# A gated recurrence in levels: the products of two levels issued as one run, one of them from copies of its operands

## The chip, the cores and the metric

The kernel runs on one core of a Trainium2 chip. The metric is the device time of one execution in microseconds; the time of a version is the median of several runs. All arithmetic is in float32, some of it in the form float32r in which a weight is split into a high and a low part and multiplied in three products. The engines are TensorE (PE in the profile, its weight loads PEld), VectorE (DVE), ScalarE (ACT), GpSimd (POOL) and SyncE (SP, which issues the DMAs).

## The reference

Two layers of a decoder trunk over 512 tokens of 1024 features. Each layer normalises, projects, runs two groups of heads side by side and projects back. The part that the change touches is the first group, a gated linear recurrence with 8 heads of 128 x 128 state:

```python
def step(state, xs):                     # one chunk; b = cumulated log decay
    qch, kch, vch, b = xs
    diff = b[:, :, :, None, :] - b[:, :, None, :, :]
    decay = jnp.where(causal, jnp.exp(jnp.where(causal, diff, 0.0)), 0.0)
    scores = jnp.einsum('bhtd,bhsd,bhtsd->bhts', qch, kch, decay)
    o = jnp.einsum('bhts,bhsv->bhtv', scores, vch)
    o = o + jnp.einsum('bhtd,bhdv->bhtv', qch * jnp.exp(b), state)
    ...
```

The second group is sliding-window attention with 16 heads. Both are gated, concatenated, projected by w_out, normalised and added to x.

## The kernel before

**Stages.** Each layer is a list of projection slabs (q, k and v of the attention, values, gates and queries of the recurrence, output gates, and the output projection in four parts: a0, a1, h0, h1). A slab's weights come in pieces of 128 x 512 over the sync queue (L163), are split on ACT (L183, the high part) and on DVE (L184, the low part), and are multiplied on TensorE (L295). `step` issues one step of a unit: three matmuls of 512 columns. At most two units run at a time, and three PSUM banks `pj` hold their sums; a unit may begin when its bank has been drained by its `evac`, on ACT or DVE (for the part a0 of the output projection: the copy to y, L901).

**Streams.** `merge` interleaves such a projection stream with a stream of other work, by the weights that the streams yield: whatever yields a larger number is followed by more projection steps. TensorE executes in the order of issue. `pin` keeps an instruction in program order; what is not pinned may be moved by the scheduler on its engine.

**The recurrence.** It is computed for four heads at a time (`hgrn(0)` and `hgrn(4)` in each layer, so four groups in all; two heads lie side by side in one "pair", a tile of 2 x 512 tokens). The lower triangle of scores is built in levels of hh = 2, 4, 8, 16, 32, 64 tokens: within each block of 2 hh tokens, the keys k of the first half meet the queries q of the second half. At each level TensorE does the products of both pairs into two PSUM banks `sc` (L764 for levels up to 16, L769 for level 32, L773 for level 64); then the halves are scaled by the decay of the neighbouring half, q on DVE (L780) and k on POOL (L781), in place, so that the next level finds its operands; and the products are moved into the tile of scores, on DVE with a mask (L788) or, for levels 32 and 64, on ACT (L793, eight pieces for both pairs; L798, four). The three `sc` banks go round. Each level issues two yields of 3.0.

**Before and behind.** `prepare(a)` makes the operands of the first diagonal blocks: for the first two heads of a group in two buffers of the tag "b" (two of them exist, 2 x 512 elements per partition each), with a reciprocal, two products and two copies (L735 to L744). `spread(a)` (L711) multiplies them. In the first merge of a layer, `prepare(2)`, `hgrn(0)` and `prepare(4)` are one chain; in the next, `prepare(6)` and `hgrn(4)`. Behind the levels come transposes of k (L807), states (L819) and outputs (L832, L835). The tag "b" is also used by the attention and by the gains of the norms (`load_g`, L366, on the sync queue).

Of the kernel before, what the change touches and what calls it, by code (L numbers as in the profile page):

```python
# [20 lines left out]
NT = SEQ // 128  # L21
# [50 lines left out]
def hybrid_kernel(ctx: ExitStack, tc: tile.TileContext, x, xt, wkv, win, wout, g_pre, g_post, lbp, ghead, sinks,  # L72
# [12 lines left out]
    def pin(ins):  # L85
        return tc.keep_in_program_order(ins)
# [8 lines left out]
    def sc():  # L95
        sc_turn[0] += 1
        return sc_tiles[sc_turn[0] % SC]

    def ac():
        ac_turn[0] += 1  # L100
        return ac_tiles[ac_turn[0] % len(ac_tiles)]
# [257 lines left out]
    def halves(tag):  # L359
        t = tmp(tag, n=2)  # L360
        return [t[:, 0], t[:, 1]]
# [73 lines left out]
    def layer(l, last):  # L435
# [310 lines left out]

        def hgrn(a):
            two = [quad.pop(a), quad.pop(a + 2)]
            bank = ac()
            spread(a, bank)  # L750
            keep_spread(a, bank)
            yield 3.0
            for hh in (2, 4, 8, 16, 32, 64):
                nb = SEQ // (2 * hh)
                per, qu = nb // NT, nb // NT // 4
                Ls = [sc(), sc()]
                for (k, q, _), L in zip(two, Ls):
                    qv = q.rearrange("p (b two j) -> p b two j", two=2, j=hh)
                    for m in range(2 * NT):
                        o_ = m * P  # L760
                        if hh <= 16:
                            for b in range(4):
                                blk, c = m * per + b * qu, m * 64 + 16 * b
                                pin(nc.tensor.matmul(L[32 * b:32 * b + 32, c:c + 16], lhsT=k[:, o_ + 32 * b:o_ + 32 * b + 32],  # L764
                                                     rhs=qv[:, blk:blk + qu, 1, :], start=True, stop=True, tile_position=(0, 32 * b)))
                        elif hh == 32:
                            for b in range(2):
                                s_, r_, c = o_ + 64 * b, 64 * b + 32 * (m % 2), m // 2 * 32
                                pin(nc.tensor.matmul(L[r_:r_ + 32, c:c + 32], lhsT=k[:, s_:s_ + 32],  # L769
                                                     rhs=q[:, s_ + 32:s_ + 64], start=True, stop=True, tile_position=(0, r_)))  # L770
                        else:
                            b, c = m % 2, m // 2 * 64
                            pin(nc.tensor.matmul(L[64 * b:64 * b + 64, c:c + 64], lhsT=k[:, o_:o_ + 64],  # L773
                                                 rhs=q[:, o_ + 64:o_ + 128], start=True, stop=True))
                for i, ((k, q, _), L) in enumerate(zip(two, Ls)):
                    h = a + 2 * i
                    qv = q.rearrange("p (b two j) -> p b two j", two=2, j=hh)
                    kv_ = k.rearrange("p (b two j) -> p b two j", two=2, j=hh)
                    tv = tots[h].rearrange("p (b two) -> p b two", two=2)
                    nc.vector.tensor_tensor(qv[:, :, 1, :], qv[:, :, 1, :], tv[:, :, 0].unsqueeze(2).broadcast_to([P, 2 * nb, hh]), op=ALU.mult)  # L780
                    nc.gpsimd.tensor_tensor(kv_[:, :, 0, :], kv_[:, :, 0, :], tv[:, :, 1].unsqueeze(2).broadcast_to([P, 2 * nb, hh]), op=ALU.mult)  # L781
                    tots[h] = sm.tile([P, 2 * nb], F32, tag=f"tot{hh}", name=f"tot{hh}", bufs=2)
                    nc.vector.tensor_tensor(tots[h], tv[:, :, 0], tv[:, :, 1], op=ALU.mult)
                    A = pairs[h].rearrange("p i t -> p (i t)")
                    if hh <= 16:
                        Av = A.rearrange("p (n b two j) -> p n b two j", n=2 * NT, two=2, j=hh)[:, :, :, 1, :]
                        mv = lmask[hh].rearrange("p (b j) -> p b j", j=hh).unsqueeze(1).broadcast_to([P, 2 * NT, per, hh])
                        nc.vector.copy_predicated(Av, mv, L.rearrange("p (n b j) -> p n b j", n=2 * NT, j=hh))  # L788
                    elif hh == 32:
                        Av = A.rearrange("p (m two t) -> p m two t", m=NT, two=2)  # L790
                        for b in range(2):
                            for e in range(2):
                                nc.scalar.copy(Av[64 * b:64 * b + 32, :, e, 64 * b + 32:64 * b + 64],  # L793
                                               L[64 * b + 32 * e:64 * b + 32 * e + 32, 0:128].rearrange("p (m t) -> p m t", m=NT))
                    else:
                        Av = A.rearrange("p (m b t) -> p m b t", m=NT, b=2)
                        for b in range(2):
                            nc.scalar.copy(Av[0:64, :, b, 64:128],  # L798
                                           L[64 * b:64 * b + 64, 0:256].rearrange("p (m t) -> p m t", m=NT))
                    yield 3.0  # L800

            kps = []
            for j in range(4):
# [430 lines left out]
```

## Time and profile before

| | |
|---|---|
| runs of the kernel before | median 909.93 us of 3, 909.6 to 910.25 |
| the profiled execution | 909.04 us |
| span of its trace | 907.3 us |
| records on L764, L769, L773 (TensorE) | 2048, 256, 128 |
| records on L711 | 512 |

A float32 product leaves two matmul records, so L769 has 32 products per group (two pairs, eight blocks of 128 tokens each, two per block), L773 has 16, and L711 and each level of L764 have 64.

A page of the profile shows busy time per engine, the granted clock of TensorE in tenths, and the chain of work that ended last. The timeline lists instructions by start, with the duration and, in brackets, the idle time of the engine before them and who ended it. "x64" at a row's end says that 64 records are merged in it. Matmuls overlap in the pipeline, so their starts tell more than their durations.

### The profile page before, as it was taken

The page shows a single profiled execution, that of the slowest core. Times are in us where ns is not written, and L with a number is a line of the kernel's source. Part 1 is how long each engine was busy: PE and PEld are TensorE (multiplying, and loading weights), DVE is VectorE, ACT ScalarE, POOL GpSimd, SP SyncE. Part 2 cuts the span into 40 slices and gives each one's busy share as a digit, 9 for nine tenths or more (in the row PEclk, how much of TensorE's full clock was granted, in tenths as well). Part 3 has the DMA queues.
Part 4 walks back from the last instruction along what each step waited for, and adds up shares of the span by engine and source line. Part 5 has one row for each costly group of instructions (what it writes and reads, how often), then busy time and mean ns, then how long its engine had stood idle before and what let it go on. Part 6 is the DMA issues. An engine that isn't in the chain of part 4 may idle for free.

```text
span 907.3 us, 18589 instructions
## 1 busy us (share of the span) xinstructions
PE 895.5 (99%) x7206; PEld 746.4 (82%) x7206; DVE 655.2 (72%) x1179; ACT 464.4 (51%) x1051; POOL 254.7 (28%) x233
## 2 busy tenths in 40 slices
PE   9999999999999999999999999999999999999997
PEld 7888888888888878887888888888888888888885
DVE  5878987989946885655787787877778457666556
ACT  7636767654656323534463376686346463135242
POOL 0135544204313122121332344550134121230102
PEclk9999999999999999999999999999999999999999
DMA  9684712322222421334356556222312323213414
GB/s 323 212 215 130 197 49 68 105 94 83 72 82 80 130 82 48 94 117 129 99 178 189 150 154 172 62 72 89 116 57 86 96 70 106 72 48 95 138 35 139
DMA packets 57144, 102.82 MB, mean 113 GB/s; under 512 B 6624, under 2 KB 9184, under 8 KB 57056
## 3 DMA queue, kind: packets, MB, share of 16 engines
q1 hardware_dynamic: 56768, 101.50, 37.0%
q8 instruction: 57, 0.93, 0.5%
q14 instruction: 31, 0.25, 0.1%
q10 hardware_dynamic: 288, 0.14, 0.1%
HBM read 89.03 MB, written 12.58 MB: 112 GB/s over the span
## 4 chain that ended last, share of the span: by engine, by line
PE 87%; DVE 7%; ACT 2%; DMA 1%; issue 1%; POOL 1%; POOLq 0%; DVEq 0%; ACTq 0%
PE pj L295 70%; PE ac L629 3%; PE sc L572 2%; PE sc L764 2%; PE sc L603 1%; PE ac L832 1%; PE ac L1060 1%; DMA raw<-in_wkv_dram 1%; DVE wlo L184 1%; PE ac L819 1%; PE ac L835 1%; PE sc L885 1%; PE sc L559 1%; DVE y L905 1%; PE sc L807 1%
## 5 line engine op out<-in xcount | busy, mean ns | idle before, releaser
L183 ACT CAST whi<-raw 128x512 fp32r<-128x512 f32 x256 | 156.0, 621 | 130.2 <-PE pj L295 118.8
L184 DVE TENSOR_TENSOR wlo<-raw,whi 128x512 fp32r<-128x512 f32 x253 | 180.8, 733 | 38.6 <-ACT whi L183 37.3
L295 PE MATMUL pj<-hhi,wlo 128*128 128x512 f32 x512 | 202.3, 396 | 0.0
L295 PE MATMUL pj<-hhi,whi 128*128 128x512 f32 x512 | 199.9, 390 | 0.0
L295 PE MATMUL pj<-hlo,whi 128*128 128x512 f32 x512 | 199.5, 390 | 0.0
L295 PE MATMUL pj<-whi,ops 128*128 128x512 f32 (+1 forms) x520 | 173.1, 395 | 0.2 <-DVE ops L865 0.2
L295 PEld LDWEIGHTS pj<-whi,ops 128*128 128x128 f32 x520 | 97.2, 188 | 20.0 <-DVE ops L865 0.6
L295 PEld LDWEIGHTS pj<-hhi,whi 128*128 128x128 f32 x512 | 96.1, 188 | 20.6
L295 PEld LDWEIGHTS pj<-hhi,wlo 128*128 128x128 f32 x512 | 96.1, 188 | 19.5
L295 PEld LDWEIGHTS pj<-hlo,whi 128*128 128x128 f32 x512 | 96.2, 188 | 18.9
L295 PE MATMUL pj<-whi,hlo 128*128 128x512 f32 x256 | 103.5, 406 | 0.3 <-DVE y L905 0.3
L295 PE MATMUL pj<-wlo,ops 128*128 128x512 f32 (+1 forms) x260 | 100.9, 388 | 0.5 <-ACT ops L864 0.5
L295 PE MATMUL pj<-wlo,hhi 128*128 128x512 f32 x256 | 100.4, 392 | 0.4 <-DVE wlo L184 0.3
L295 PE MATMUL pj<-whi,hhi 128*128 128x512 f32 x256 | 100.3, 392 | 0.0
L781 POOL TENSOR_TENSOR k<-k,tot 128x512 f32<-128x512 f32 x40 | 57.5, 1456 | 115.1 <-PE sc L764 45.9
L590 ACT ACTIVATE s<-sc,negm 128x128 f32<-128x128 f32 x128 | 45.6, 368 | 37.5 <-DVE negm L583 35.2
L295 PEld LDWEIGHTS pj<-wlo,ops 128*128 128x128 f32 x260 | 49.0, 188 | 9.5 <-ACT ops L864 0.9
L295 PEld LDWEIGHTS pj<-whi,hhi 128*128 128x128 f32 x256 | 48.1, 188 | 10.4
L295 PEld LDWEIGHTS pj<-wlo,hhi 128*128 128x128 f32 x256 | 48.3, 189 | 8.9 <-DVE wlo L184 1.2
L295 PEld LDWEIGHTS pj<-whi,hlo 128*128 128x128 f32 x256 | 48.2, 188 | 8.6 <-DVE y L905 0.7
L597 POOL TENSOR_TENSOR s<-s,sums 128x512 f32<-128x512 f32 x32 | 35.2, 1101 | 51.7 <-DVE sums L595 27.7
L780 DVE TENSOR_TENSOR q<-q,tot 128x512 f32<-128x512 f32 x40 | 41.7, 1056 | 10.7 <-PE sc L769 4.7
(209 smaller groups left out, 1383.8 us busy)
## 6 DMA issues: line engine op xcount, KB each, us to landing
raw<-in_win_dram SPq DMA_DIRECT2D x192, 256.0 KB, 2.8
raw<-in_wout_dram SPq DMA_DIRECT2D x64, 256.0 KB, 2.7
stack<-rot SPq DMA_DIRECT2D x16, 512.0 KB, 3.4
qs<-stack SPq DMA_DIRECT2D x32, 256.0 KB, 4.7
xs<-in_xt_dram SPq DMA_DIRECT2D x8, 256.0 KB, 4.4
raw<-in_wkv_dram SPq DMA_DIRECT2D x8, 256.0 KB, 4.1
a<-in_x_dram SPq DMA_DIRECT2D x8, 256.0 KB, 3.9
x_mid<-a SPq DMA_DIRECT2D x8, 256.0 KB, 3.4
```

Of the source, the lines that this page charges most:

```text
L183: keep(nc.scalar.copy(hi, v))
L184: keep((nc.gpsimd if i in on_pool and i % 2 else nc.vector).tensor_tensor(lo, v, hi.bitcast(F32), op=ALU.subtract))
L295: nc.tensor.matmul(u.o, lhsT=u.sta(k, u.w)[i], rhs=u.mov(k, u.w)[j], start=(n == 0), stop=(n == len(u.list) - 1))
L559: pin(nc.tensor.matmul(S[:, h * P:(h + 1) * P], lhsT=q[:, h, t_], rhs=kst[v][p][:, 0:P], start=(h == 0 and p == 0), stop=(h == 3 and p == 1)))
L572: pin(nc.tensor.matmul(S[:, h * 256:(h + 1) * 256], lhsT=q[:, 2 * hp_ + h, t_], rhs=kst[v][p][:, (n - 1) * P:(n + 1) * P], start=(h == 0 a ...
L590: nc.scalar.activation(pt[:, h * P:(h + 1) * P], cur[h], AF.Exp, bias=negm[:, h:h + 1], scale=SCALE, accum_out=sums[:, h:h + 1])
L597: nc.gpsimd.tensor_tensor(pv, pv, sums.unsqueeze(2).broadcast_to([P, 4, P]), op=ALU.mult)
L603: pin(nc.tensor.transpose(T[:, h * P:(h + 1) * P], pt[:, h * P:(h + 1) * P], ident))
L629: pin(nc.tensor.matmul(U, lhsT=vst[v][:, blk, :], rhs=d, start=(i == 0), stop=(i == len(terms) - 1)))
L764: pin(nc.tensor.matmul(L[32 * b:32 * b + 32, c:c + 16], lhsT=k[:, o_ + 32 * b:o_ + 32 * b + 32], rhs=qv[:, blk:blk + qu, 1, :], start=True ...
L780: nc.vector.tensor_tensor(qv[:, :, 1, :], qv[:, :, 1, :], tv[:, :, 0].unsqueeze(2).broadcast_to([P, 2 * nb, hh]), op=ALU.mult)
L781: nc.gpsimd.tensor_tensor(kv_[:, :, 0, :], kv_[:, :, 0, :], tv[:, :, 1].unsqueeze(2).broadcast_to([P, 2 * nb, hh]), op=ALU.mult)
```

## The change

At level 32 nothing is multiplied any more. ACT copies the first halves of k and the second halves of q of each pair into a buffer of the tag "b" (`kept`, one for each pair: 128 x 512 elements of k, as many of q), and the scaling of k and q goes on. At level 64 the 16 products of that level are issued as before, and behind them, in the same run, the 32 products of level 32, from the copies. They go into columns 256 to 383 of the same two banks, and all twelve evacuations of ACT follow there. The yields are 2.0 at level 32 and 4.0 at level 64 instead of 3.0 at each, so that their sum stays.

```diff
         def hgrn(a):
             two = [quad.pop(a), quad.pop(a + 2)]
+            kept = []
...
-                Ls = [sc(), sc()]
+                Ls = [sc(), sc()] if hh != 32 else [None, None]
                 for (k, q, _), L in zip(two, Ls):
+                    if hh == 32:
+                        kept.append(halves("b"))
+                        for t, x, e in zip(kept[-1], (k, q), (0, 1)):
+                            nc.scalar.copy(t.rearrange("p (b j) -> p b j", j=hh), x.rearrange("p (b two j) -> p b two j", two=2, j=hh)[:, :, e, :])
+                        continue
...
-                        elif hh == 32:
-                            for b in range(2):
-                                s_, r_, c = o_ + 64 * b, 64 * b + 32 * (m % 2), m // 2 * 32
-                                pin(nc.tensor.matmul(L[r_:r_ + 32, c:c + 32], lhsT=k[:, s_:s_ + 32],
-                                                     rhs=q[:, s_ + 32:s_ + 64], start=True, stop=True, tile_position=(0, r_)))
                         else:
                             b, c = m % 2, m // 2 * 64
                             pin(nc.tensor.matmul(L[64 * b:64 * b + 64, c:c + 64], lhsT=k[:, o_:o_ + 64],
                                                  rhs=q[:, o_ + 64:o_ + 128], start=True, stop=True))
+                if hh == 64:
+                    for (k, q), L in zip(kept, Ls):
+                        for m in range(2 * NT):
+                            for b in range(2):
+                                s_, r_, c = 64 * m + 32 * b, 64 * b + 32 * (m % 2), 256 + m // 2 * 32
+                                pin(nc.tensor.matmul(L[r_:r_ + 32, c:c + 32], lhsT=k[:, s_:s_ + 32], rhs=q[:, s_:s_ + 32],
+                                                     start=True, stop=True, tile_position=(0, r_)))
...
-                    elif hh == 32:
+                    elif hh == 64:
                         Av = A.rearrange("p (m two t) -> p m two t", m=NT, two=2)
                         for b in range(2):
                             for e in range(2):
                                 nc.scalar.copy(Av[64 * b:64 * b + 32, :, e, 64 * b + 32:64 * b + 64],
-                                               L[64 * b + 32 * e:64 * b + 32 * e + 32, 0:128].rearrange("p (m t) -> p m t", m=NT))
-                    else:
+                                               L[64 * b + 32 * e:64 * b + 32 * e + 32, 256:384].rearrange("p (m t) -> p m t", m=NT))
                         Av = A.rearrange("p (m b t) -> p m b t", m=NT, b=2)
...
-                    yield 3.0
+                    yield {32: 2.0, 64: 4.0}.get(hh, 3.0)
```

Lines behind the edit move by up to seven: the levels up to 16 are L770 now, level 64 is L774 and the products from the copies are L781, the copies themselves L762, the scalings L788 and L789, the evacuations L801 and L805, the y copy L908.

How the order of instructions moves is shown in two places of the first group of the first layer. First TensorE, before: the run of level 32 between steps of the projections (`pj` are their banks, `sc2` and `sc0` two of the three banks of the recurrence).

```order
L295 MATMUL pj_2751<-hlo_122,whi_2582 128x512
L295 MATMUL pj_2751<-hhi_121,whi_2582 128x512
L769 MATMUL sc2_80<-q_1933,k_1803 32x32 x16
L769 MATMUL sc0_78<-q_2126,k_2032 32x32 x16
L295 MATMUL pj_2865<-whi_2710,ops_2228 128x512
```

And the run of level 64, which stands 33 projection matmuls behind it:

```order
L295 MATMUL pj_2976<-wlo_2604,ops_2227 128x512
L295 MATMUL pj_2976<-whi_2603,ops_2227 128x512
L773 MATMUL sc1_79<-q_1933,k_1803 64x64 x8
L773 MATMUL sc2_80<-q_2126,k_2032 64x64 x8
L295 MATMUL pj_2953<-whi_2725,ops_2228 128x512
```

Now, the joined run (`b` are the two buffers of copies):

```order
L295 MATMUL pj_2927<-wlo_2604,ops_2227 128x512
L295 MATMUL pj_2927<-whi_2603,ops_2227 128x512
L774 MATMUL sc2_80<-q_1933,k_1803 64x64 x8
L774 MATMUL sc0_78<-q_2126,k_2032 64x64 x8
L781 MATMUL sc2_80<-b_2893 32x32 x16
L781 MATMUL sc0_78<-b_2896 32x32 x16
L295 MATMUL pj_2911<-whi_2725,ops_2228 128x512
```

It stands 21 projection matmuls behind the place that the run of level 32 left, and 45 ahead of the transposes of k; one run of projections is no longer cut.

Second, ACT, before, from the conversions ahead of level 32 to the first y copies (`k_2626` and `q_2854` belong to the heads that `prepare(4)` prepares, `a` are the tiles of scores, `y` takes the output projection):

```order
L688 ACTIVATE f_2625<-f_2625,lb_b_136,lb_a_135 128x512
L738 COPY b_3378<-k_2626 128x256
L183 CAST whi_2871<-raw_2723 128x512
L183 CAST whi_2886<-raw_2830 128x512
L696 ACT_TABLE_LOAD
L696 ACTIVATE q_2854<-q_2854 128x512
L736 COPY b_3338<-q_2854 128x256
L793 COPY a_1983<-sc2_80 32x4x32 x4
L793 COPY a_2168<-sc0_78 32x4x32 x4
```

Now the same place, where the four copies stand and no evacuation:

```order
L688 ACTIVATE f_2625<-f_2625,lb_b_136,lb_a_135 128x512
L762 COPY b_2893<-k_1803 128x512
L762 COPY b_2893<-q_1933 128x512
L762 COPY b_2896<-k_2032 128x512
L762 COPY b_2896<-q_2126 128x512
L183 CAST whi_2871<-raw_2723 128x512
L183 CAST whi_2886<-raw_2830 128x512
L696 ACT_TABLE_LOAD
L696 ACTIVATE q_2854<-q_2854 128x512
```

And further on, now, behind the joined run:

```order
L908 COPY y_2918<-pj_2865 128x512
L801 COPY a_1983<-sc2_80 32x4x32 x4
L805 COPY a_1983<-sc2_80 64x4x64 x2
L801 COPY a_2168<-sc0_78 32x4x32
L908 COPY y_2995<-pj_2911 128x512
L801 COPY a_2168<-sc0_78 32x4x32 x3
L805 COPY a_2168<-sc0_78 64x4x64 x2
L736 COPY b_3344<-q_2854 128x256
L738 COPY b_3344<-k_2626 128x256
L183 CAST whi_3023<-raw_2869 128x512
L908 COPY y_3016<-pj_2927 128x512
```

The twelve evacuations stand together around the second y copy, and the copies of `prepare(4)` (L736, L738), two of which stood ahead of or between the evacuations, have gone behind them, since their buffers are taken until the joined run has read them. On DVE the reciprocals and products of `prepare(4)` and on POOL its two L742 move behind the scalings of level 64 in the same way. On the sync queue the loads of the norm gains into "b" (L366), which waited for the second group's `spread`, now stand behind thirteen more weight loads and wait for the second group's joined run.

## The prediction

> **What bounds the kernel now.** I read the page first, then the lists of waits, then the timelines of the engines around one group of four heads.
>
> ```profile
> span 907.3 us, 18589 instructions
> PE 895.5 (99%) x7206; PEld 746.4 (82%) x7206; DVE 655.2 (72%) x1179; ACT 464.4 (51%) x1051; POOL 254.7 (28%) x233
> PEclk9999999999999999999999999999999999999999
> PE 87%; DVE 7%; ACT 2%; DMA 1%; issue 1%; POOL 1%; POOLq 0%; DVEq 0%; ACTq 0%
> ```
>
> TensorE (PE) is busy in 99% of the span, its granted clock stays in the top tenth throughout, and 87% of the chain that ended last is its own work. So the change is worth what it does to TensorE's row of matmuls, unless it makes TensorE wait for someone. The lists of waits (who for whom, us in total, times, longest) say how near that is:
>
> ```profile
> POOL k L781 <- PE sc L769: 22.7, 4, 6.4
> PE sc L1037 <- DVE u L1028: 1.5, 1, 1.5
> PE pj L295 <- ACT ops L864: 0.5, 1, 0.5
> ```
>
> POOL stands 22.7 us before the products that are moved, but that costs nothing, since nobody on TensorE waits for POOL there. TensorE's own longest wait is 1.5 us, at the start, and 0.5 us later on.
>
> **What a run of products costs TensorE.** Its timeline in the first group of the first layer (start, duration, engine, line, count):
>
> ```profile
> 236.19 0.39 PE L295 MATMUL pj<-whi,ops 128*128 128x512 f32 x1
> ...
> 238.68 0.39 PE L295 MATMUL pj<-hhi,whi 128*128 128x512 f32 x1
> 239.00 0.76 PE L769 MATMUL sc<-q,k 128*32 128x32 f32 x64
> 239.69 0.50 PE L295 MATMUL pj<-whi,ops 128*128 128x512 f32 x1
> 240.03 0.39 PE L295 MATMUL pj<-wlo,ops 128*128 128x512 f32 x1
> ...
> 241.65 0.62 PE L295 MATMUL pj<-whi,ops 128*128 128x512 f32 x2
> ```
>
> Durations overlap, so only starts count. Projection matmuls (L295) start every 0.226 us: the eleven steps from 236.19 to 238.68 take 2.49. From the last one before the run (238.68) to the second behind it (240.03) pass 1.35 us, of which two ordinary steps are 0.45. The run of level 32 (32 products, 64 records) therefore costs **0.90 us**. Afterwards the seven steps from 240.03 to 241.65 take 1.62, 0.231 each: some 0.04 us more goes into a slow stretch behind the run.
>
> How much of the 0.90 is fixed? The diagonal spread (L711) has twice as many products of the same form, 64, and level 64 (L773) has 16 of 64 columns:
>
> ```profile
> 197.86 0.39 PE L295 MATMUL pj<-hhi,whi 128*128 128x512 f32 x1
> 198.17 0.73 PE L711 MATMUL ac<-b 128*32 128x32 f32 x62
> ...
> 199.44 0.50 PE L295 MATMUL pj<-hhi,wlo 128*128 128x512 f32 x1
> 199.78 0.40 PE L295 MATMUL pj<-hlo,whi 128*128 128x512 f32 x1
> 247.14 0.39 PE L295 MATMUL pj<-whi,ops 128*128 128x512 f32 x1
> 247.45 1.15 PE L773 MATMUL sc<-q,k 128*64 128x64 f32 x32
> 248.54 0.50 PE L295 MATMUL pj<-whi,ops 128*128 128x512 f32 x1
> 248.87 0.39 PE L295 MATMUL pj<-wlo,ops 128*128 128x512 f32 x1
> ```
>
> By the same count L711 costs 1.92 - 0.45 = 1.47 and L773 1.73 - 0.45 = 1.28. Thirty-two more products of the form of L769 cost 1.47 - 0.90 = 0.57, so 0.90 - 0.57 = **0.33 us is the fixed price** of going into a run and out of it.
>
> **The change part by part.** *TensorE.* No product disappears: the 32 of level 32 now read the copies and stand directly behind the 16 of level 64. What goes is one entry and one exit per group (four groups: two per layer). What comes is one change inside the run, from tiles 64 columns wide to tiles 32 wide; no row shows it. Its bounds are 0 (products simply follow products; then 0.33 is saved) and 0.33 (as dear as an exit and an entry together; then nothing is). It is one change of form where exit and entry are two, so I take half, 0.16. With the one slow stretch that also goes: 0.16 + 0.04 = 0.20 per group, **0.8 us in four groups**.
>
> The Trainium skill, page "TensorEngine Tiling (Array Packing)", section "Key Properties", says that changing the tiling mode, and not merely the tile, drains the TensorE. That speaks against the full saving: four changes of mode per group become three. By the rule the sum is a quarter of the two fixed prices, 0.16 per group; by a count of runs alone it would be 0.33. The step of 0.32 instead of 0.226 us from 238.68 to 239.00 agrees that a change of mode costs something.
>
> *ScalarE (ACT)* gets 16 copies, four per group. Nearest rows: a conversion of the same 128x512 elements, and the evacuations that now stand together:
>
> ```profile
> 232.15 0.80 ACT L688 ACTIVATE f<-f,lb_b,lb_a 128x512 f32<-128x512 f32 x1
> 232.85 0.41 ACT L738 COPY b<-k 128x256 f32<-128x256 f32 x1
> ...
> 239.54 2.14 ACT L793 COPY a<-sc 32x128 f32<-32x128 f32 x8 [0.79 <-PE sc L769]
> 241.70 0.62 ACT L183 CAST whi<-raw 128x512 fp32r<-128x512 f32 x1
> ...
> 248.19 1.52 ACT L798 COPY a<-sc 64x256 f32<-64x256 f32 x4
> 249.73 0.59 ACT L901 COPY y<-pj 128x512 f32<-128x512 f32 x1
> ```
>
> At 0.62 us a copy (bounds 0.6 and 0.8 by these rows) that is 2.5 us per group and 10 us in all, on an engine that is idle 49% of the span: nothing, as long as nothing behind it in its queue is late. Are the operands there? The copies need level 16's scaled k from POOL and q from VectorE (DVE):
>
> ```profile
> 230.90 2.93 POOL L781 TENSOR_TENSOR k<-k,tot 128x512 f32<-128x512 f32 x2 [2.71 <-PE sc L764]
> 233.44 0.94 DVE L780 TENSOR_TENSOR q<-q,tot 128x512 f32<-128x512 f32 x1
> 241.01 2.15 DVE L780 TENSOR_TENSOR q<-q,tot 128x512 f32<-128x512 f32 x2
> ```
>
> The second k is ready at 233.8, the second q at 234.4; ACT's queue reaches the copies at about 232.9 and ends them at 235.4. The scalings of level 32 follow (2.15 on DVE, about 2.9 on POOL): done by about 238. The joined run comes 21 projection matmuls behind the old place of L769, at 238.68 + 22 x 0.226 + 0.09 = 243.7. TensorE has some 5 us to spare and will not wait for the copies.
>
> *ACT behind the joined run.* Twelve evacuations now stand together (2.14 + 1.52 = 3.7 us), and the projections' y copies (L901) between and behind them. First bank full at about 245.1; the four L793 and two L798 of it end at 246.9, one L793 and the next y copy at 247.8, the other five evacuations at 249.4; then two copies of prepare (0.41 each), a conversion (0.62) and the third y copy, which ends at about 251.4 (before: 250.3). Its bank is written again by the unit that starts with the second matmul of this row, 253.43, less the 0.2 saved:
>
> ```profile
> 253.20 0.61 PE L295 MATMUL pj<-whi,ops 128*128 128x512 f32 x2
> ```
>
> 1.8 us to spare. The cover is thinner by 1.3 us than it was, and each microsecond beyond it would be one of TensorE's.
>
> *What waits for the "b" buffers.* The kept copies take the two buffers that prepare(4) had used early. Its reciprocals, products and POOL's two L742 move behind the joined run, and so do weight splits (L184) behind them on DVE:
>
> ```profile
> 234.93 1.74 DVE L735 RECIPROCAL b<-f 128x256 f32<-128x256 f32 x1
> 248.80 1.54 DVE L184 TENSOR_TENSOR wlo<-raw,whi 128x512 fp32r<-128x512 f32 x1
> 264.35 0.40 PE L295 MATMUL pj<-hhi,wlo 128*128 128x512 f32 x1
> ```
>
> Two reciprocals and their products put the split of 248.80 back by 2 to 4 us; the slab that it belongs to is first read at 264.35. Nothing. On the sync engine's queue (SP) the loads of the norm gains into "b" move behind thirteen weight loads and wait for the second group's joined run (about 360):
>
> ```profile
> 307.54 0.81 SPq L366 DMA_DIRECT2D b<-in_g_post_dram  x2
> 337.63 31.98 SPq L163 DMA_DIRECT2D raw<-in_wout_dram  x8
> 364.68 0.62 ACT L183 CAST whi<-raw 128x512 fp32r<-128x512 f32 x1 [0.53 <-PE pj L295]
> ```
>
> They stand behind the fifth of those eight loads. The sixth waits for a conversion that comes at 364.7, so the hole is there already. Nothing either.
>
> **Sum.** 0.8 us off the profiled execution's own 909.04 gives 908.2; off the 909.93 of the runs, which lie 0.9 higher, **909.1**.
>
> **Rivals.** *The inner change is free*: all of 0.33 + 0.04 goes, 4 x 0.37 = 1.5, 908.4. For it: products of one form follow each other without a gap; against it: the step into a run is 0.09 us too long. *It costs as much as exit and entry*: only the slow stretch goes, 0.16, 909.8. For it: the new weights have another width and another source than those before. *The products hide under level 64's*: 4 x 0.90 = 3.6, 906.3; against it, TensorE issues one after the other, and no row shows two forms side by side. *ACT's queue becomes the wait*: copies stand in order, so a late q on DVE holds everything behind them. The place is groups one and three, where y copies drain the projections' banks; it decides from 1.8 us of further delay on. In the second layer ACT drains q itself, behind the copies, and DVE's second scaling of q begins late:
>
> ```profile
> 682.80 1.28 ACT L696 ACT_TABLE_LOAD   x1
> 685.97 0.60 ACT L696 ACTIVATE q<-pj 128x512 f32<-128x512 f32 x1 [1.89 <-PE pj L295]
> 686.23 0.68 DVE L780 TENSOR_TENSOR q<-q,tot 128x512 f32<-128x512 f32 x1
> ```
>
> The copy of that q cannot start before 686.9, the table load (1.28) and L696 come after it, some 3 us later than now. If such delays run 1.5 us past the cover in both groups, that is 2 x 1.5 = 3.0 against the gain: 912.1, slower than before. Against it stands the slack worked out above.
>
> **How the numbers follow.** Forecast 0.47; inner change free 0.20, as dear as two 0.20; hidden products 0.05; ACT's queue 0.08. A measurement of this kernel tells about 0.2% (1.8 us) from no change: below 908.1 is faster, above 911.75 slower. The first three cases are all within it: 0.87. Hidden products make faster 0.05, ACT's queue slower 0.08. The range takes in the three cases and 0.2 to 0.5 us at each end, for runs that lie otherwise and small waits: 908.2 to 910.3.
>
> **What would show it.** The joined run, counted as above, should cost 0.90 + 1.28 - 0.16 = 2.0 us (1.85 if the inner change is free, 2.2 if it saves nothing). The step into the run and out of it should be as before, and the projections around it at 0.226. TensorE's busy time should not fall much more than the span. Wrong would be: a gap of TensorE ahead of a projection unit within 15 us behind a joined run, released by ACT; a joined run that starts late, released by ACT or POOL; or POOL's wait for it beyond what its queue had.

## The result, and the profile after

| | runs | median us | range us |
|---|---|---|---|
| before, on the same chip | 13 | 909.60 | 908.50 to 910.31 |
| changed | 13 | 907.51 | 906.93 to 908.91 |

The ratio is 0.9981, with a 95% interval of 0.9974 to 0.9988: the changed kernel is 2.1 us faster, 1.1 to 2.4 by the interval. The forecast was a gain of 0.8 us (909.1, range 908.2 to 910.3). The sign was right, and the gain was more than twice as large. The time lies below the range.

The page of the changed kernel, the rows that answer to those of before:

```profile
span 905.3 us, 18588 instructions
PE 893.1 (99%) x7206; PEld 746.8 (83%) x7206; DVE 652.1 (72%) x1179; ACT 471.7 (52%) x1067; POOL 255.4 (28%) x233
PEclk9999999999999999999999999999999999999999
PE 87%; DVE 6%; issue 3%; ACT 2%; POOL 1%; DMA 0%; POOLq 0%; DVEq 0%; ACTq 0%
```

TensorE has the same 7206 records, the clock is as before, and TensorE's busy time is 2.4 us shorter, as the span is 2.0 shorter. ACT has 16 copies more and is busy 7 us longer. The chain's share of DMA, 1% before, is 0%. TensorE's waits (who for whom, us in total, times, longest):

```profile
PE sc L1044 <- DVE u L1035: 1.5, 1, 1.5
PE sc L393 <- DVE xn L388: 1.1, 2, 0.7
...
PE pj L295 <- ACT ops L871: 0.5, 1, 0.5
PE pj L295 <- DVE wlo L184: 0.3, 1, 0.3
```

No wait for ACT's y copies (L908) or for POOL is among them. The joined run on TensorE's timeline, first group of the first layer:

```profile
236.04 0.39 PE L295 MATMUL pj<-hhi,whi 128*128 128x512 f32 x1
...
243.52 0.39 PE L295 MATMUL pj<-whi,ops 128*128 128x512 f32 x1
243.84 1.15 PE L774 MATMUL sc<-q,k 128*64 128x64 f32 x32
244.92 0.76 PE L781 MATMUL sc<-b 128*32 128x32 f32 x64
245.61 0.50 PE L295 MATMUL pj<-whi,ops 128*128 128x512 f32 x1
245.95 0.39 PE L295 MATMUL pj<-wlo,ops 128*128 128x512 f32 x1
```

From 243.52 to 245.95 pass 2.43 us, less two steps of 0.2275: the run costs **1.975 us**, where two runs cost 0.895 + 1.275 before. The 33 steps ahead of it, from 236.04 to 243.52, take 7.48, or 0.2267 each; they begin with the 21st matmul behind the run of level 16. Before, a run of level 32 stood among them, and the 31 steps behind that run (240.03 to 247.14, rows quoted in the prediction) took 7.11, which is 0.08 more than 31 ordinary ones. They are not slow throughout (first three rows before, last row changed):

```profile
242.11 0.39 PE L295 MATMUL pj<-wlo,ops 128*128 128x512 f32 x1
...
243.70 0.63 PE L295 MATMUL pj<-whi,ops 128*128 128x512 f32 x2
...
245.78 0.62 PE L295 MATMUL pj<-whi,ops 128*128 128x512 f32 x2
```

```profile
248.01 0.39 PE L295 MATMUL pj<-wlo,ops 128*128 128x512 f32 x1
```

The nine steps from 240.03 to 242.11 take 2.08 (0.231 each), the next seven 1.59 (0.227), then nine again 2.08, and the last six 1.36 (0.227). So a slow stretch lasts about ten steps, costs some 0.04 us and is over; the second one here has no run ahead of it, and no row shows what began it. Behind the joined run the nine steps from 245.95 to 248.01 take 2.06, which is 0.02 beyond ordinary ones. ACT at the same place:

```profile
232.56 0.62 ACT L762 COPY b<-k 128x512 f32<-128x512 f32 x1 [0.47 <-POOL k L789]
233.09 0.61 ACT L762 COPY b<-q 128x512 f32<-128x512 f32 x1
234.06 0.62 ACT L762 COPY b<-k 128x512 f32<-128x512 f32 x1 [0.35 <-POOL k L789]
234.58 0.62 ACT L762 COPY b<-q 128x512 f32<-128x512 f32 x1
...
245.45 1.06 ACT L801 COPY a<-sc 32x128 f32<-32x128 f32 x4 [2.94 <-PE sc L781]
246.53 0.74 ACT L805 COPY a<-sc 64x256 f32<-64x256 f32 x2
...
250.79 0.59 ACT L908 COPY y<-pj 128x512 f32<-128x512 f32 x1
```

The copies are done at 235.2, nearly ten microseconds ahead of their readers, and the third y copy ends at 251.38.

**Where the time went, stretch by stretch.** Single matmul starts of TensorE's timeline cut the span into stretches that hold the same work in every version: from one `spread` to the next, to the transposes of zh, the gated output of the recurrence (L885 before, L892 now), to the transposes in the norm of the second layer (L393). The table has three profiled executions of the kernel before (the last two from the experiments) and two of the changed one, in us:

| stretch | before, three executions | changed, two executions |
|---|---|---|
| A: 1st `spread` to 2nd (group 1) | 108.80, 108.80, 108.77 | 108.46, 108.45 |
| B1: to the second transposes of zh (group 2) | 58.87, 58.90, 58.91 | 58.58, 58.59 |
| B2: to the fifth (no products of a group) | 51.01, 50.58, 50.09 | 50.10, 50.10 |
| C1: to the last L393 | 45.62, 45.61, 45.60 | 45.90, 45.90 |
| C2: to the 3rd `spread` (attention, second layer) | 186.52, 186.48, 186.48 | 186.16, 186.15 |
| D: 3rd `spread` to 4th (group 3) | 108.96, 108.95, 108.81 | 108.66, 108.69 |
| E: to the transposes of zh (group 4) | 57.66, 57.80, 57.75 | 57.40, 57.42 |

A, B1, D and E hold the four groups and lose 0.34 + 0.31 + 0.23 + 0.33 = **1.2 us**. The forecast had 0.8 there. B2, C1 and C2 hold no product of the change; by the means they give -0.46 + 0.29 - 0.34 = **-0.5 us**, which the forecast didn't have at all. So two things had to be found out: why joining gives 1.2, and what B2 is. What stands ahead of the first `spread` takes 197.9 to 200.1 us in the nineteen profiles (198.3 and 200.1 in two of one kernel), so a span or a time also moves by that. (The expectations below call the end of B2 the fourth transposes of zh; it is the fifth group of them, at 416.85 us in the kernel before.)

In B2 the profiled execution of before has this on TensorE:

```profile
408.22 0.39 PE L295 MATMUL pj<-whi,hhi 128*128 128x512 f32 x1
408.88 0.50 PE L295 MATMUL pj<-whi,hlo 128*128 128x512 f32 x1 [0.28 <-DVE y L905]
...
411.06 0.39 PE L295 MATMUL pj<-whi,hlo 128*128 128x512 f32 x1
411.48 0.50 PE L295 MATMUL pj<-wlo,hhi 128*128 128x512 f32 x1
```

Two starts are 0.66 and 0.42 apart where 0.2275 is usual, 0.6 us lost, and 0.9 in all with slow steps behind both (B2 is 50.1 without them). The cause is a chain on the other engines (sync queue, ACT, DVE):

```profile
402.24 0.38 SPq L163 DMA_DIRECT2D raw<-in_wkv_dram  x1
402.71 0.42 SPq L938 DMA_DIRECT2D a<-in_x_dram  x1
...
406.29 0.62 ACT L183 CAST wkv<-raw 128x512 fp32r<-128x512 f32 x1 [1.31 <-DMA raw<-in_wkv_dram]
...
406.94 0.69 DVE L184 TENSOR_TENSOR wkv<-raw,wkv 128x512 fp32r<-128x512 f32 x1 [2.04 <-ACT wkv L183]
...
408.15 0.68 DVE L905 TENSOR_TENSOR y<-pj,y 128x512 f32<-128x512 f32 x1
```

The third piece of wkv (a weight of the next layer) lands 4.05 us behind its issue. Its conversion, its low part on DVE and the y sum behind that in DVE's queue are late, and the y sum frees the bank that TensorE wants. In the changed kernel the same load is issued at 401.30 and converted at 404.21.

### The profile page after: what moved, and what is told of

Read it like the earlier page. It is cut to its first block, busy times and chain, and to the rows that moved or that the text cites. A ratio compares the mean times of both kernels' runs of the same rounds, so it can differ in the third digit from the quotient of the medians.

```text
span 905.3 us, 18588 instructions
## 1 busy us (share of the span) xinstructions
PE 893.1 (99%) x7206; PEld 746.8 (83%) x7206; DVE 652.1 (72%) x1179; ACT 471.7 (52%) x1067; POOL 255.4 (28%) x233
## 4 chain that ended last, share of the span: by engine, by line
PE 87%; DVE 6%; issue 3%; ACT 2%; POOL 1%; DMA 0%; POOLq 0%; DVEq 0%; ACTq 0%
PE pj L295 71%; PE ac L629 3%; PE sc L572 2%; PE sc L770 2%; PE ac L839 2%; PE sc L603 1%; PE ac L842 1%; PE ac L826 1%; DVE wlo L184 1%; PE sc L892 1%; PE sc L559 1%; PE sc L814 1%; PE ac L711 1%; DVE a L973 1%; DVE y L912 0%
## 5 line engine op out<-in xcount | busy, mean ns | idle before, releaser
L789 POOL TENSOR_TENSOR k<-k,tot 128x512 f32<-128x512 f32 x40 | 58.3, 1480 | 108.3 <-PE sc L770 51.9
L788 DVE TENSOR_TENSOR q<-q,tot 128x512 f32<-128x512 f32 x40 | 37.4, 946 | 20.3 <-PE sc L774 10.9
```

## The experiments

Medians are compared with the kernel before in the same session (909.1 to 909.3 us in all of them).

### Both kernels again, and the join taken apart

> The kernel before, unchanged, with a second trace. In the first trace TensorE loses 0.9 us (gaps of 0.43 and 0.19 us beyond the usual start to start, and a slow stretch) near 408 us, where the fourth load of the next layer's wkv weights lands late and holds VectorE's queue. Theory A, landing luck: that gap belongs to the execution and not to the kernel; this trace may lack it or have it elsewhere, and its span then goes with it (without it about 906.3 us). Theory B, the change removes it by its order: the gap stands here again at the same place with about the same length, and the span is about 907.3.

> The changed kernel, unchanged, with a second trace. Theory A: the direct gain is 0.3 us per group, 1.2 in all (ratio about 0.9987), and the rest of the first difference comes and goes; this trace may show a gap near 407 us. Theory B: no gap near 407 us, ratio about 0.9977, 2.1 us. In both the joined run costs 1.98 us in the first layer's first group.

Measured: 909.26, ratio 1.0001 (0.9992 to 1.0009), and 907.62, ratio 0.9982 (0.9974 to 0.9991), a gain of 1.7 us. The stall was there again in the kernel before, half as long (B2 50.58), and not in the changed one (50.10). That looked like theory B; the third profile of the kernel before, further below, speaks against it.

`e1_apart` keeps the copies and the places of all else, and puts the products back into a run of their own (and their evacuation with it):

```diff
-                Ls = [sc(), sc()] if hh != 32 else [None, None]
+                Ls = [sc(), sc()]
...
-                if hh == 64:
+                if hh == 32:
                     for (k, q), L in zip(kept, Ls):
...
-                    yield {32: 2.0, 64: 4.0}.get(hh, 3.0)
+                    yield 3.0
```

> As the changed kernel with its copies and its use of the b buffers, but the products of level 32 form a run of their own at their old place again, and its evacuations follow there. If joining the runs is what gains: the direct gain is gone, about +1.2 us against the changed kernel, ratio to the kernel before 0.999 to 1.001. If the copies (POOL and VectorE need no longer wait for TensorE, the b buffers held longer, the loads of the gains moved) are what gains: it stays 1 us or more faster than the kernel before, ratio about 0.998.

Measured: 908.2, ratio 0.9992 (0.9983 to 1.0001). Its runs cost 0.885 and 1.285, as before. Stretches A, B1, D and E lie within 0.15 us of those of before: what they lose in the changed kernel comes with the join, not with the copies. By its time alone this run lies between the two cases, 1.1 us below the kernel before and 0.6 above the changed one: its profile has no stall (B2 50.09) and a C2 as short as the changed kernel's (186.12).

`e1_turns` lets the products of both levels take turns inside the joined run, one of level 64, two of level 32, so that it has 31 changes of width instead of one:

```diff
+                            if hh == 64:
+                                kk, qq = kept[[id(x[0]) for x in two].index(id(k))]
+                                for b in range(2):
+                                    s_, r_, c = 64 * m + 32 * b, 64 * b + 32 * (m % 2), 256 + m // 2 * 32
+                                    pin(nc.tensor.matmul(L[r_:r_ + 32, c:c + 32], lhsT=kk[:, s_:s_ + 32], rhs=qq[:, s_:s_ + 32],
...
-                if hh == 64:
-                    for (k, q), L in zip(kept, Ls):
```

> As the changed kernel, but inside the joined run the 16 products of level 64 and the 32 of level 32 alternate (one, then two): 31 changes of tile width per run in place of one, all else the same. If each change costs what the first trace leaves for it, 0.13 us (fixed price 0.33 less the 0.20 that a joined run saved): a run of 1.98 + 30 x 0.13 = 5.9 us, and about 15 us more in all, 923 us. If a change of width inside a run is free: runs of 1.98 us and no difference, 907.5 us. If TensorE can even overlap products of the two widths: shorter runs, below 1.9 us.

Measured: 930.59, ratio 1.0243 (1.0227 to 1.0259). TensorE's timeline, the ends of the run:

```profile
243.88 0.39 PE L295 MATMUL pj<-whi,ops 128*128 128x512 f32 x1
244.20 0.33 PE L774 MATMUL sc<-q,k 128*64 128x64 f32 x2
244.46 0.26 PE L780 MATMUL sc<-b 128*32 128x32 f32 x4
244.64 0.33 PE L774 MATMUL sc<-q,k 128*64 128x64 f32 x2
...
251.10 0.26 PE L780 MATMUL sc<-b 128*32 128x32 f32 x4
251.29 0.50 PE L295 MATMUL pj<-whi,ops 128*128 128x512 f32 x1
251.62 0.40 PE L295 MATMUL pj<-wlo,ops 128*128 128x512 f32 x1
```

The run costs 7.74 - 0.455 = 7.285 us. Thirty more changes cost 7.285 - 1.975 = 5.31, **0.177 us each**. The expectation had 0.13 for a change and so a time of 923 us; the prediction had taken 0.16 between 0 and 0.33. The Trainium skill's page "TensorEngine Tiling (Array Packing)", section "Key Properties", says that a change of the tiling mode drains the TensorE. This run agrees that a change costs time, and gives the price; whether a drain is what costs it, no row shows.

### The width change taken away

`e2_narrow` computes level 64 in tiles that are 32 columns wide too, 32 products of 64 columns instead of 16, so that the joined run has one width throughout; `e3_narrow_apart` does the same to the kernel before, in the old place:

```diff
-                            b, c = m % 2, m // 2 * 64
-                            pin(nc.tensor.matmul(L[64 * b:64 * b + 64, c:c + 64], lhsT=k[:, o_:o_ + 64],
-                                                 rhs=q[:, o_ + 64:o_ + 128], start=True, stop=True))
+                            for b in range(2):
+                                r_, c = 64 * (m % 2) + 32 * b, m // 2 * 64
+                                pin(nc.tensor.matmul(L[r_:r_ + 32, c:c + 64], lhsT=k[:, o_ + 32 * b:o_ + 32 * b + 32],
+                                                     rhs=q[:, o_ + 64:o_ + 128], start=True, stop=True, tile_position=(0, r_)))
```

> The changed kernel with the products of level 64 in tiles 32 columns wide too (32 products of 64 columns of q in place of 16, same sums), so that the joined run has no change of width inside. If a change of width is what keeps a joined run from saving the whole fixed price (0.177 us each by the run with alternating widths): the run loses that, and its 32 new products cost between 0.57 us (price per product, as for the 32 of level 32) and 1.14 (price per column), where the 16 now cost about 0.95: runs of 1.4 to 2.0 us in place of 1.98, ratio to the kernel before 0.9958 to 0.9983. If the widths do not matter: 2.0 to 2.2 us.

> The kernel before, with the 16 products of level 64 cut into 32 of tiles 32 columns wide (64 columns each), in their own run at the old place. It tells whether the 0.15 us that the joined run saved with such products come from the missing change of width or from the products themselves. Theory A, the change of width: the run of level 64 by itself costs as before, 1.24 to 1.30 us, and the time is that of the kernel before, ratio 0.9995 to 1.0005. Theory B, the products: it costs about 1.12 us, 0.6 us less in four groups, ratio 0.9993.

> The changed kernel with the products of level 64 in tiles 32 columns wide, once more beside the others of this call. If it is really 0.6 to 0.8 us better than the changed kernel by the missing change of width (four times 0.15 us), it gives about 906.6 to 906.9 (ratio 0.997 to 0.9975); if the time of 906.48 was luck, 907.5 (0.998). In the trace the joined run should cost 1.82 us again, and no stall near 408 us should appear.

Measured: `e2_narrow` 906.48, ratio 0.997 (0.9958 to 0.9981), and again 906.69, 0.9973 (0.9963 to 0.9983); `e3_narrow_apart` 908.13, 0.9989 (0.9979 to 0.9998). The joined run with narrow products, and behind it the run of level 64 alone in the kernel before:

```profile
243.52 0.39 PE L295 MATMUL pj<-whi,ops 128*128 128x512 f32 x1
243.84 1.10 PE L775 MATMUL sc<-q,k 128*32 128x64 f32 x64
244.76 0.77 PE L782 MATMUL sc<-b 128*32 128x32 f32 x64
245.46 0.50 PE L295 MATMUL pj<-whi,ops 128*128 128x512 f32 x1
245.80 0.40 PE L295 MATMUL pj<-wlo,ops 128*128 128x512 f32 x1
```

```profile
247.26 0.39 PE L295 MATMUL pj<-whi,ops 128*128 128x512 f32 x1
247.58 1.10 PE L774 MATMUL sc<-q,k 128*32 128x64 f32 x64
248.61 0.50 PE L295 MATMUL pj<-whi,ops 128*128 128x512 f32 x1
248.95 0.40 PE L295 MATMUL pj<-wlo,ops 128*128 128x512 f32 x1
```

The first costs 2.28 - 0.455 = 1.825, 0.15 less than the changed kernel's. The second costs 1.69 - 0.455 = 1.235, only 0.04 less than the 1.275 of wide products, although there are twice as many. So 0.11 of the 0.15 is the missing change, and 0.04 the products. With one width the join saves 0.895 + 1.235 - 1.825 = 0.305 a group, about the whole fixed price of 0.33; with two widths it saves 0.195. This version beats both kernels: by 0.8 to 1.1 us the changed one's 907.5 to 907.6. In times, `e3_narrow_apart` gained more (1.0 us, 0.2 to 1.9) than its four runs can (0.2); its two profiles (the second is `e4_apart_again`, one run of 908.85) are free of the stall near 408 us, of which below.

### What moves along: the gains' loads, prepare(4), the copies

Three kernels before, with side effects of the change alone. `e2_gains_late` takes the buffers "b" at level 64 of a layer's second group with two one-column copies, so that the gains' loads (L366) move behind it; `e2_prepare_late` does that in the first group, so that prepare(4) moves; `e2_idle_copies` has the 16 copies, which nobody reads; they take the same buffers, so here prepare(4) and the gains' loads move too (the loads from 308 to 347 us).

```diff
+                    if hh == 64 and a == 4:
+                        nc.scalar.copy(halves("b")[0][:, 0:1], k[:, 0:1])
```

```diff
+                    if hh == 64 and a == 0:
+                        nc.scalar.copy(halves("b")[0][:, 0:1], k[:, 0:1])
```

```diff
+                    if hh == 32:
+                        for t, x, e in zip(halves("b"), (k, q), (0, 1)):
+                            nc.scalar.copy(t.rearrange("p (b j) -> p b j", j=hh), x.rearrange("p (b two j) -> p b two j", two=2, j=hh)[:, :, e, :])
```

> The kernel before, with one thing added: in the second group of each layer, at level 64, ACT copies one column of k into each of the two b buffers (four copies of 128 x 1 in all), which nothing reads. So the loads of the norm gains into these buffers move behind thirteen more weight loads, as in the changed kernel; runs, copies and prepare(4) stay as before. Theory C (the place of the gain loads on the sync queue decides how late the next layer's third wkv load lands): no gap of TensorE near 408 us, 51.0 or 50.6 us from the second to the fourth gate transposes become 50.1, ratio about 0.9993 (0.5 to 0.9 us). Theory D (it is something else, copies or shifts): 50.6 to 51.0 again, ratio 1.000.

> As the run with the gains late, but the two one-column copies stand in the first group of each layer only: prepare(4) moves behind level 64 of the first group, and the loads of the gains keep their old place. Theory C: the gap near 408 us is there, 50.6 to 51.0 us between those transposes, ratio 1.000. Theory D: the gap may be gone. In both the first group (108.80 us from one spread to the next before) should not change by more than 0.1.

> The kernel before with the 16 copies of the changed kernel added at level 32, which nothing reads; all products as before, from k and q, in runs of their own. If the copies cost nothing: runs as before, and a ratio of 1.000 or, with the gain loads moved (theory C), 0.9993. If they get in ACT's way: above 1.001, with waits of TensorE for ACT's y copies.

Measured: 909.23, ratio 0.9999 (0.999 to 1.0008); 910.23, 1.0011 (1.0002 to 1.002); 909.05, 0.9995 (0.9986 to 1.0004). The copies cost nothing, as forecast. `e2_prepare_late` lost 1.1 us; its stretch A is 1.1 us longer (109.90), and not by prepare(4). ACT and TensorE there:

```profile
242.96 0.19 ACT L759 COPY b<-k 128x1 f32<-128x1 f32 x1 [0.76 <-POOL k L783]
...
244.66 0.58 ACT L903 COPY y<-pj 128x512 f32<-128x512 f32 x1
```

```profile
244.01 0.39 PE L295 MATMUL pj<-whi,ops 128*128 128x512 f32 x1
245.30 0.50 PE L295 MATMUL pj<-whi,ops 128*128 128x512 f32 x1 [0.90 <-ACT y L903]
```

My one-column copy reads the second pair's k and stands in ACT's queue until POOL has scaled it. The y copy behind it is late, and TensorE starts 1.29 us after the last matmul instead of 0.23. That is the prediction's rival on ACT's queue, at another place, with its price: the copies of the changed kernel escape it because they wait for POOL 0.47 and 0.35 us only, and no y copy stands close behind them.

`e2_gains_late` had no stall in B2 (50.12), but `e2_idle_copies`, with late loads as well, had one (51.04), so the loads' place did not decide it alone. The next run put the loads back in the changed kernel, by giving the second group's copies other buffers:

```diff
-                        kept.append(halves("b"))
+                        kept.append(halves("b") if a == 0 else [tmp("s"), tmp("u" if kept else "s")])
```

> The changed kernel, but the copies of the second group of each layer lie in buffers of the tags s and u instead of b, so that the loads of the norm gains (L366) go back to the place that they have before the change; everything else stays. Theory A: the stall of TensorE near 408 us, which the traces with early gain loads show and those with late ones mostly don't, comes with the early loads. Then it is back here (the starts of two projection matmuls 0.4 to 0.7 us apart, one or two times between 407 and 413 us, the stretch from the second to the fourth transposes of zh 50.5 to 51.0 us instead of 50.1), and the time is 0.5 to 0.9 us above the changed kernel's: about 908.2, ratio 0.9989. Theory B: the stall does not hang on these loads. Then the stretch stays at 50.1 and the time at about 907.5, ratio 0.998.

Measured: 907.6, ratio 0.9986 (0.9977 to 0.9995), and B2 is 50.09. Theory A of that run fell: the loads stand where they stood before, and the stall stays away.

### The stall near 408 us

An x load is issued 0.47 us behind the late wkv load (row above), and its data are read only at 439 us. `e4_x_late` makes the first four x loads wait for a sum of y by a one-column copy, so that the four wkv loads go alone:

```diff
                 hT2["x"] = halves("a")
                 for c in range(2):
+                    if l == 0 and tt < 2:
+                        nc.scalar.copy(hT2["x"][c][:, 0:1], yt[NT - 1][:, 1, 0:1])
```

> The kernel before, but the first four loads of x for the last output projection of the first layer (L938, at 391 to 408 us, read only at 439 us) wait for a one-column copy by ACT of a sum of y, so that they go behind the four wkv loads instead of between them. Theory D: the third wkv load lands late in the kernel before (3.7 to 4.3 us behind its issue) because the x load that is issued 0.47 us behind it shares the DMA engines. Then it lands 2.7 to 2.9 us after its issue here, TensorE shows no two starts of projection matmuls over 0.4 us apart between 400 and 415 us, the stretch from the second to the fourth transposes of zh is 50.0 to 50.1 us instead of 50.6 to 51.0, and the time is 0.5 to 0.9 us below that of before (ratio 0.999 to 0.9995). Theory E: the landing is late for another reason. Then the stretch stays at 50.6 to 51.0 and the ratio at 1.

> The same edit on the changed kernel with narrow products of level 64. There the third wkv load lands in 2.7 to 2.8 us already and no stall is seen near 408 us. If that stall is all that the x loads cost, nothing changes: 906.5 to 906.7 us (ratio 0.997 to 0.9973). If the loads disturb more than that, up to 0.5 us below.

> The kernel before, a third look. If the late third wkv load belongs to this kernel, the stretch from the second to the fourth transposes of zh is 50.5 to 51.0 us again; if it comes and goes from run to run, it has an even chance to be 50.1.

> The kernel before with the products of level 64 in narrow tiles in their own run, a second look. If its free stretch (50.04 us) belongs to the kernel, it is 50.0 to 50.1 again; if it comes and goes from run to run, it may be 50.5 to 51.0.

Measured: `e4_x_late` 908.59, ratio 0.9993 (0.9984 to 1.0002); with narrow products 906.51, 0.9968 (0.9956 to 0.9981). B2 is 50.09 and 50.04, and the third wkv load, issued at 400.87, is converted without a wait at 403.58:

```profile
400.87 0.37 SPq L163 DMA_DIRECT2D raw<-in_wkv_dram  x1
...
403.58 0.62 ACT L183 CAST wkv<-raw 128x512 fp32r<-128x512 f32 x1
```

But the third profile of the unchanged kernel before had no stall either (B2 50.09, one run of 908.39), with the x load right behind the wkv load:

```profile
402.16 0.38 SPq L163 DMA_DIRECT2D raw<-in_wkv_dram  x1
402.64 0.42 SPq L938 DMA_DIRECT2D a<-in_x_dram  x1
...
405.10 0.62 ACT L183 CAST wkv<-raw 128x512 fp32r<-128x512 f32 x1 [0.19 <-DMA raw<-in_wkv_dram]
```

So the same load in the same kernel landed 4.05, 3.66 and 2.94 us behind its issue in three executions: **the stall comes and goes from run to run.** It was there in two of three profiles of the kernel before, in `e2_prepare_late` and `e2_idle_copies` (50.92 and 51.04), and not in `e2_gains_late` and `e1_apart` or in either profile of the kernel before with narrow products (50.04 and 50.05).

What goes with it is the landing. In the fifteen profiles with the x loads in their old place the third wkv load is converted 2.68 to 4.27 us behind its issue. The four with a stall are those with 3.66 us or more, and in the eleven others, up to 3.38 us, TensorE loses nothing in B2. Without the x loads it is 2.70 to 2.85 us in all four profiles. What makes it late is not shown: with the x load right behind it, it mostly lands in time as well.

With the x loads away no profile has it, so the last pair measures the join by itself:

> The kernel before with the four x loads behind the wkv loads, once more, as the base for the next run: no stall near 408 us, stretch from the second to the fourth transposes of zh 50.0 to 50.1 us, 908.4 to 908.8 us.

> The changed kernel with the four x loads behind the wkv loads. Here and in the run above nothing can stall near 408 us, so the difference of the two is what the joined runs are worth by themselves. My account (0.84 us in the runs, some 0.35 us in the stretches behind them): 1.2 us, so 907.2 to 907.5 us where the base is 908.4 to 908.8, and in the trace 1.2 us between the sums of the four stretches with a group's products. The rival, that all of the measured 2.1 us belongs to the join and the stall is an accident of the profiles: 906.4 to 906.6.

Measured: 908.41 (ratio 0.9988, 0.9979 to 0.9997) and 906.8 (0.9975, 0.9964 to 0.9986). The spans are 907.0 and 905.8. The stretches A, B1, D and E are shorter by 0.33 + 0.32 + 0.25 + 0.31 = 1.21 us, and B2, C1 and C2 agree within 0.02 us. By the trace the join is worth 1.2 us. By the medians it is 1.6, below the expected 907.2 to 907.5 and above the rival's 906.4 to 906.6; each median is uncertain by about 0.9 us to either side, so the times alone don't decide, and the stretches do.

## Why the prediction was right and wrong, step by step

**That TensorE bounds the kernel**, and that the change is worth what it does to TensorE's row: right. No run shows another engine as the bound.

**The fixed price of a run, 0.33 us**: right. Joined with one width, a group saves 0.305.

**The change of width inside the run, 0.16 us**: right within its spread, though half of the bounds was a choice without a row, and that it came so close is in part luck. `e1_turns` gives 0.177 as a mean of both directions, the changed kernel 0.33 - 0.195 = 0.135, the narrow products 0.11. The joined run costs 1.975 where 2.0 was forecast. The four runs together save 0.20 + 0.20 + 0.27 + 0.20 = 0.87 us instead of 0.64 (in the second and fourth group the transposes of zh, 0.45 us, are taken off, since the joined run stands right behind them): each a little more, and the third group's L769 had cost 0.96 instead of 0.89.

**The slow stretch behind a run, 0.04 us**: the size of one stretch was read rightly, but the term in the sum was half of what it should have been, since it counted one stretch per group. The steps beyond 0.2267 us behind the runs of levels 32 and 64, and behind the transposes of zh in the second and fourth group, add up to 0.40, 0.41 and 0.47 us in the three profiles before, to 0.37 in `e1_apart`, and to 0.09 in both profiles of the changed kernel. That is 0.33 us in four groups, where 0.16 stood in the sum. In the second and fourth group two stretches go, because the joined run now stands right behind the transposes; in the first, the second bump shown above goes with the run of level 32 (`e1_apart` has that run and no bump). So the join gives 0.87 + 0.33 = 1.2 us instead of 0.8; both terms of the sum were too small.

**ACT's copies hidden**: right (`e2_idle_copies`). **The third y copy at 251.4, 1.8 us to spare**: right, it ends at 251.38 and TensorE doesn't wait. **The rival on ACT's queue**: did not happen, though `e2_prepare_late` shows that it is real and costs 1.1 us once.

**TensorE's longest wait, "0.5 us later on"**: misread. The list before also has `PE sc L393 <- DVE xn L388: 0.8, 2, 0.7`; the sum did not use it, but C1 moved just there.

**Buffers "b", prepare(4) and the gains' loads, "nothing"**: right for the gains' loads, in both directions. For prepare(4) alone there is no clean run, since the one that moved it also held ACT; the changed kernel shows no wait behind it.

**The steps that failed** are two. The first is TensorE's term, "0.8 us in four groups": the runs save 0.87 instead of 0.64, and the slow stretches 0.33 instead of 0.16, so it is 1.2. The second is the sum, which took all that lies outside the four groups as unchanged. There B2, C1 and C2 moved by -0.46, +0.29 and -0.34 us in the means of the table. What B2 lost is the stall. Of the nine profiles without a joined run and with the x loads in their old place four have one, of 0.5 to 0.9 us; of the six such profiles with a joined run none has. That it is rarer there may be chance; no run shows a reason. Together the account is 1.2 + 0.46 - 0.29 + 0.34 = 1.7 us, against 2.1 (1.1 to 2.4) in the first comparison and 1.7 in the second; the 0.4 between them has no place in a profile and lies within the interval. The base, too, was 0.3 lower: 909.6 in the measured pair, 909.93 in the runs that the forecast started from.

Open stay the causes of C1 and C2. In C1, TensorE waits longer for the norm before the second layer (L393, 1.1 instead of 0.8 us in the lists of waits), in all profiles with a joined run, but not when the x loads are away. The difference stands at one step, POOL's part of the norm (L356): it begins 0.36 us behind DVE's L354 instead of 0.07. C2 is 0.2 to 0.4 us shorter in all profiles with copies, joined or not, with the x loads away, and in `e2_prepare_late`; there, two runs of the attention's products (L572) start without a delay of 0.1 to 0.2 us. What ties these to the edits wasn't found. They nearly cancel.

## What to carry to other kernels

Going from large matmuls into a run of small ones and back costs a fixed sum, here 0.33 us and another 0.02 to 0.06 in some ten matmuls behind it. Joining runs saves nearly all of the 0.33 (0.305) where the joined products have one tile width, here even at the price of twice as many products, and 0.20 where they have two. Count every slow stretch that goes, also those of other small runs that come to stand right beside the joined one. And before an effect of two tenths of a per cent is forecast off one profile, look for pauses of the bounding engine that have nothing to do with the change: take a second profile of the same kernel, or cut both into stretches of equal work.

## What the runs showed of the hardware beside that

- A change between tiles 64 and 32 columns wide costs TensorE 0.177 us, as a mean of both directions (`e1_turns`), and 0.11 to 0.135 from 64 to 32 in the joined run; and 32 products of 32 x 64 columns take no longer than 16 of 64 x 64 (1.235 and 1.275 us with entry and exit).
- Behind a run of small products some ten large matmuls start about 0.230 us apart instead of 0.2267, 0.02 to 0.06 us in all, and then every 0.2267 us again; the granted clock shows no difference. In the first group of the kernel before such a stretch also stands 16 steps behind a run, from 243.70 us on.
- The same load of 256 KB, at the same place of the same program, was converted 2.94 to 4.05 us behind its issue in three executions of the kernel before, with another load issued 0.47 us behind it (2.68 to 4.27 in all fifteen profiles with that load there); with that load away it took 2.70 to 2.85 in four.
